# One inference step of a streaming encoder layer on one Trainium2 core: running sums two steps behind their loads, decay factors three steps later in the first group, the second norm's rows stored by ScalarE, and another input for an early Silu

## The chip, the core and the metric

The kernel runs on one core of one Trainium2 chip. The metric is the time of one execution on the device, in microseconds (us). A profile of one execution shows, for each engine, when it worked and what ended each of its waits: TensorE (PE, matmuls; PEld, its weight loads), VectorE (DVE), ScalarE (ACT), GpSimd (POOL) and SyncE (SP), whose queue issues most of the transfers.

## What is computed

One layer for 2048 prompt tokens and 64 sample tokens, 1024 features, everything in float32. `layer` of the reference, cut to its course:

```python
mod = (c_act @ w_ada + b_ada)[:, None, :]
sh1, sc1, gt1, sh2, sc2, gt2 = jnp.split(mod, 6, -1)
h = rmsnorm(x, g1) * (1 + sc1) + sh1
u, q, k, v, o, gates = jnp.split(h @ w_in, cuts, -1)
pool_out, pool_buf_new = pool_mixer(u, pool_buf, start, w_pool, s_pool)
hs, C, n, m = mlstm_seq(q, k * HEAD_DIM ** -0.5, v, ig, lf, C, n, m)   # 4 heads, chunks of tokens
hs = hs * lax.rsqrt(jnp.mean(hs * hs, -1, keepdims=True) + EPS) * g_head * jax.nn.sigmoid(o)
x = x + gt1 * (jnp.concatenate([pool_out, hs], -1) @ w_out)
h2 = rmsnorm(x, g2) * (1 + sc2) + sh2
up = h2 @ w_up                      # then a causal conv of width 3, halves a and g
x = x + gt2 * ((jax.nn.silu(g) * a) @ w_down)
y = rmsnorm(x, g_final)
```

## The kernel before

Tokens run along the free dimension. The first part (the attention half) takes four groups of tokens, 512 each, the last with the 64 sample tokens as well. Every matrix product is made of three passes over operands that are split in a high and a low part, so TensorE has most of the work.

A group goes through the projection of v and the gates (`proj_v`), four heads of q, k and o (`proj_qko`), four pooling projections and the output projection (`outproj`). Beside these matmuls run smaller pieces of work, each written as a generator. They stand in lists `bg[0]` to `bg[5]`, and `gemm` takes the next step of one of them (`tick(i)`) at fixed places among its matmuls. A `yield` in a generator is the end of such a step, so one more `yield` puts what follows one step later. A list is a queue: what is behind a generator in its list waits until it is done. `drain(i)` takes all that is left of a list at once. In the attention half, behind group 0's first projections, a scheduler of the framework then orders each engine's instructions by when it thinks that they can start, so the program's order is not quite the engines'. In the second half (FFN) the written order of the compute engines stands.

The pieces that matter here:

- `ada` (lines 175 to 230) makes one of the modulation vectors per group (the sample's and the prompt's) as running sums on VectorE: 16 blocks of `w_ada` (128x512) are loaded into tiles `raw` by SP (line 192), and each is multiplied into two accumulators (line 205 for a new pair, line 207 else), 32 instructions. Later groups (`first=False`) load three blocks ahead, and the block three further behind each step. There are four tiles `raw`, so a fifth load waits until the sums of the first block are done. It stands in `bg[3]`, three ticks to a projection.
- `up_sums` (lines 866 to 902, `bg[4]`) adds and subtracts blocks of `w_up` (lines 892 to 896) and stores them (`wsum`, line 881, SP) for the FFN.
- `gate_rows` (lines 1167 to 1244, `bg[0]`) turns the gates into decay factors: `CL` by a transpose (line 1229), a copy (line 1233) and three exponentials (line 1235), and four yields later `GL` by a matmul (line 1241) and a copy (line 1242). Right after the first head's three projections stands `drain(0)` (line 1455).
- `lstm` (lines 1265 to 1356) is one head's memory: `at` (lines 1278, 1281, 1300), `kw` (line 1289), the states `st` (line 1314) and the output `nd` (lines 1320 to 1323).
- `norm_h` (lines 730 to 749, `bg[1]` of the last group) normalizes the first FFN group's rows: it loads sixteen half rows of `x2d` into ten tiles (line 738), scales and shifts each (line 726 on VectorE, line 728 on ScalarE) and stores it to `h2d` (line 746, SP). Half rows 10 to 15 go into tiles whose first content must have been stored.

SP's queue is in order: a transfer that waits (for a tile to come free, or for the result that it stores) holds back all behind it. Besides the named ones it carries the weights that TensorE takes, `hl_kept` to `wt` (line 374), 512 KB each.

Between the halves, line 1970 runs a Silu on one column of `V`, into a column of `RF` that later work overwrites; its result is not used. The first Silu whose result is used is that of line 1665. ScalarE must have the table of a function loaded before it runs (ACT_TABLE_LOAD). `V` holds the small vectors and is loaded at the kernel's start; `UC` (line 1495) is a tile of the FFN that GpSimd sets to zero (line 1496).

Of the kernel before, what the change touches and what calls it, by code (L numbers as in the profile page):

```python
# [11 lines left out]
AF = mybir.ActivationFunctionType  # L12
# [14 lines left out]
FH = FT // 2  # L27
# [36 lines left out]
def tile_layer(ctx: ExitStack, tc: tile.TileContext, xT, vecs, cst, rst, rowv, w_mod, w_ada, w_qkou, w_v, w_pool,  # L64
               w_out, w_up, w_down, w_quad, st_C, st_pool, yT, o_pool, o_C, o_m, o_conv):
    nc = tc.nc
    act, dve, pool, pe = nc.scalar, nc.vector, nc.gpsimd, nc.tensor
# [19 lines left out]
    def m2_ps():  # L87
        return bank("m2")
# [9 lines left out]
    def scr():  # L98
        return sp.tile([P, TMAX], F32, tag="scr", name="scr")
# [22 lines left out]
    def big(tile):  # L122
        return tile.bitcast(F32).rearrange("p a t -> p (a t)")
# [11 lines left out]
    V = cp.tile([P, NV], F32, tag="V", name="V")  # L135
# [27 lines left out]
    def raw_tile():  # L163
        return wp.tile([P, WN], F32, tag="raw", name="raw", bufs=RB)
# [10 lines left out]
    def ada(m, first):  # L175


        todo = [(j, k) for j in range(2) for k in range(KD)]
        src = [w_ada[m - 2, k, :, j * 512:(j + 1) * 512] for j, k in todo]
        got = {}  # L180

        def load(i):
            if first:

                if i % 2 == 0 and i < len(todo):
                    w = a1.tile([P, 4, 256], F32, tag="w4", name="w4", bufs=5).rearrange("p (a b) c -> p a (b c)", a=2)
                    for d in range(2):
                        got[i + d] = w[:, d]
                        tc.keep_in_program_order(nc.sync.dma_start(out=w[:, d], in_=src[i + d]))
            elif i < len(todo):  # L190
                got[i] = raw_tile()[:, :512]
                nc.sync.dma_start(out=got[i], in_=src[i])
        lead = 4 if first else 3
        for i in range(lead):
            load(i)
        yield
        accs = []
        for i, (j, k) in enumerate(todo):
            if k == 0:
                acc = [a1.tile([P, 512], F32, tag="acc", name="acc", bufs=4) for _ in range(2)]  # L200
                accs += acc
            w = got.pop(i)
            for s in range(2):
                if k == 0:
                    dve.tensor_scalar(out=acc[s], in0=w, scalar1=CA[:, k, s:s + 1], scalar2=None, op0=ALU.mult)
                else:
                    dve.scalar_tensor_tensor(out=acc[s], in0=w, scalar=CA[:, k, s:s + 1], in1=acc[s],  # L207
                                             op0=ALU.mult, op1=ALU.add)
            load(i + lead)
            yield  # L210
        yield

        pt = m2_ps()
        for c, acc in enumerate(accs):
            pe.matmul(pt[32 * c:32 * c + 32, :], ones[:, 0:32], acc, start=True, stop=True)
        MR = scr()
        dve.tensor_copy(MR[:, :512], pt)
        yield
        yield
        pt = m2_ps()  # L220
        for n in range(4):
            pe.transpose(pt[:, n * P:(n + 1) * P], MR[:, n * P:(n + 1) * P], ident)
        for j in range(2):
            bia = V[:, V_BA + m * 8 + 4 * j:V_BA + m * 8 + 4 * j + 4]
            dve.tensor_tensor(out=MOD[:, m, 4 * j:4 * j + 4],
                              in0=pt.rearrange("p (n c t) -> p n c t", n=4, c=4)[:, :, 2 * j:2 * j + 2, 0],
                              in1=bia.unsqueeze(2).broadcast_to([P, 4, 2]), op=ALU.add)
        if m == 4:
            scale_cols(G2, V_G2, 4, 0, KD)
        yield  # L230

    def scale_cols(G, v0, m, k0, n):
        dve.scalar_tensor_tensor(out=G[:, k0:k0 + n], in0=MOD[:, m, k0:k0 + n], scalar=1.0,
                                 in1=V[:, v0 + k0:v0 + k0 + n].unsqueeze(2).broadcast_to([P, n, 2]),
                                 op0=ALU.add, op1=ALU.mult)
# [6 lines left out]
    for g in range(NG):  # L242
        o = Grp()
# [219 lines left out]
    def mx_tile(k):  # L463
        return beside(mx, "mx", k)
# [91 lines left out]
    h2d = dr.tile([KD, P, FT], F32, tag="h2d", name="h2d")  # L556
# [3 lines left out]
    RF = cp.tile([P, 16], F32, tag="RF", name="RF")  # L560
# [71 lines left out]
    for g in range(NFG):  # L632
        o = Grp()
# [87 lines left out]
    def normed(x, k, t0, w, rb):  # L721

        for (a, b, s) in ((t0, min(t0 + w, TP), 0), (max(t0, TP), t0 + w, 1)):
            if a < b:
                a, b = a - t0, b - t0
                dve.scalar_tensor_tensor(out=x[:, a:b], in0=x[:, a:b], scalar=G2[:, k, s:s + 1], in1=rb[:, a:b],  # L726
                                         op0=ALU.mult, op1=ALU.mult)
                act.activation(x[:, a:b], x[:, a:b], AF.Identity, bias=sh2(k, s))

    def norm_h(o, rows, scr):  # L730

        todo = [(t0, k) for t0 in (o.t0, o.t0 + FH) for k in range(KD)]
        xs = []

        def load(i):
            t0, k = todo[i]
            xs.append(rows[i % 10])
            nc.sync.dma_start(out=xs[i], in_=x2d[k, :, t0:t0 + FH])
        for i in range(8):
            load(i)  # L740
        box = []
        for h in range(2):
            yield from bcast_cols(RS2, o.t0 + h * FH, FH, box, lambda dt=F32: rows[10 + h] if dt == "rb" else scr(dt))
        for i, (t0, k) in enumerate(todo):
            normed(xs[i], k, t0, FH, box[i // KD])
            nc.sync.dma_start(out=h2d[k, :, t0:t0 + FH], in_=xs[i])
            yield
            if i > 1 and i + 6 < len(todo):
                load(i + 6)
# [109 lines left out]
    if True:  # L859
# [44 lines left out]
        def rows_of(o):  # L904

            xs = []
            for k in range(0, KD, 2):
                t = big(mx_tile(k))
                for i in (0, 1):
                    xs.append(t[:, i * TMAX:i * TMAX + o.T])  # L910
                    if o.g > 1:
                        nc.sync.dma_start(out=xs[-1], in_=xT[k + i, :, o.t0:o.t0 + o.T])
            return xs
# [253 lines left out]
        def gate_rows(o, gt, cols):  # L1167
# [58 lines left out]
            for (a, b, n, s) in o.tsegs:  # L1226
# [3 lines left out]
                for qn in range(4):  # L1230
# [2 lines left out]
                        dve.tensor_copy(CL[:n, a:b, qn, :], src)  # L1233
                    else:
                        act.activation(CL[:n, a:b, qn, :], src, AF.Exp)
            for _ in range(4):
                yield
            pb = m2_ps()
            for (a, b, n, s) in o.tsegs:
# [184 lines left out]
        for o in groups:  # L1424
# [3 lines left out]
            if o.g > 0:  # L1428
                bg[3].append(ada(2 + o.g, False))
                tick(3)  # L1430
# [15 lines left out]
            if o.last:  # L1446
                xs = [t[:, j * FH:(j + 1) * FH] for t in [big(mx_tile(k)) for k in range(4)] for j in range(3)]
            else:
                xs = rows_of(groups[o.g + 1])
# [45 lines left out]
    UC = f1.tile([P, 2 * NF, 2], F32, tag="UC", name="UC")  # L1495
# [471 lines left out]
    ET = mybir.EngineType  # L1967
    fctx.enter_context(tc.manual_schedule(engines={ET.PE, ET.Activation, ET.DVE, ET.Pool}))
    x3, ssum = [], None
    act.activation(RF[:, 0:1], V[:, 0:1], AF.Silu)  # L1970
    bg[5].append(down_sums())
    for o in fgroups:
        Bo = B[o.g]
# [244 lines left out]
```

## Time and profile before

| What | Value |
|---|---|
| time, median of 3 (lowest to highest) | 2201.76 us (2200.48 to 2202.48) |
| the profiled execution: its time, its span | 2205.02 us, 2203.2 us |
| granted clock of TensorE, mean over the span | 0.996 |
| PEld busy | 2067.4 us |
| DMA engines, moved bytes and mean rate | 521.67 MB, 237 GB/s |
| L442, matmuls of the attention half (out of `hl`) | 397.5 us busy, 1920 instructions |
| L207, running sums on VectorE, `raw` tiles | 60.5 us busy, 84 instructions, 29.2 us idle before them |
| L1547, matmuls of the FFN's first products | 889.7 us busy, 5544 instructions |

The profile covers one execution. Its span runs from the first instruction to the last, and the 1.8 us around it (2205.02 - 2203.2) belong to no instruction. A row of the groups names the line, the engine, the operation, `out<-in` and the shapes, then how often, the busy time, the mean duration in ns, and the idle time of the engine just before these instructions with what ended it. Durations of matmuls overlap, so the distance between two starts says more than the sum of durations.

The groups of tokens start (first matmul of `proj_v`) at about 222 us (group 1), 404 us (group 2) and 590 us (group 3); the FFN's first product of its first pair ends at about 809 us.

### The profile page before, as it was taken

The page shows a single profiled execution, that of the slowest core. Times are in us where ns is not written, and L with a number is a line of the kernel's source. Part 1 is how long each engine was busy: PE and PEld are TensorE (multiplying, and loading weights), DVE is VectorE, ACT ScalarE, POOL GpSimd, SP SyncE. Part 2 cuts the span into 40 slices and gives each one's busy share as a digit, 9 for nine tenths or more (in the row PEclk, how much of TensorE's full clock was granted, in tenths as well). Part 3 has the DMA queues.
Part 4 walks back from the last instruction along what each step waited for, and adds up shares of the span by engine and source line. Part 5 has one row for each costly group of instructions (what it writes and reads, how often), then busy time and mean ns, then how long its engine had stood idle before and what let it go on. Part 6 is the DMA issues. An engine that isn't in the chain of part 4 may idle for free. (4 is left out here: it accounts for less than half of the span.)

```text
span 2203.2 us, 38338 instructions
## 1 busy us (share of the span) xinstructions
PE 2178.9 (99%) x13708; PEld 2067.4 (94%) x13708; DVE 1630.4 (74%) x2996; ACT 1038.8 (47%) x2024; POOL 262.1 (12%) x546
## 2 busy tenths in 40 slices
PE   8999999999999999999999999999999999999998
PEld 7888888888899999999999999999999999999998
DVE  4887659577765768787958677676757597888885
ACT  3553335244343446464636444545435356554454
POOL 0010001001000100000101220101111331121112
PEclk9999999999999999999999999999999999999999
DMA  9977986997898686667646877777569786665562
GB/s 336 357 251 257 340 287 230 321 325 244 287 327 271 208 298 221 207 199 243 208 157 215 294 230 235 232 208 220 180 185 277 219 247 179 182 175 181 157 200 79
DMA packets 304191, 521.67 MB, mean 237 GB/s; under 512 B 27480, under 2 KB 131288, under 8 KB 304000
## 3 DMA queue, kind: packets, MB, share of 16 engines
q1 hardware_dynamic: 283008, 482.74, 67.0%
q10 hardware_dynamic: 11776, 28.09, 3.4%
q0 software_dynamic: 9216, 8.39, 3.0%
q8 instruction: 108, 1.77, 0.3%
q14 instruction: 83, 0.68, 0.1%
HBM read 408.36 MB, written 127.52 MB: 243 GB/s over the span
## 5 line engine op out<-in xcount | busy, mean ns | idle before, releaser
L1547 PE MATMUL mm<-hx,wt 128*128 128x352 f32 x5544 | 889.7, 321 | 3.0 <-DVE wt L388 1.5
L1547 PEld LDWEIGHTS mm<-hx,wt 128*128 128x128 f32 x5544 | 880.3, 188 | 7.5 <-DVE wt L388 4.3
L442 PE MATMUL mm<-hl,wt 128*128 128x512 f32 (+2 forms) x1920 | 397.5, 359 | 2.0 <-DMA wt<-hl_kept 2.0
L2061 PE MATMUL mm<-av,wt 128*128 128x352 f32 (+2 forms) x2400 | 385.2, 321 | 0.4 <-DVE av L1701 0.3
L385 ACT ACTIVATE wt<-raw 128x512 fp32r<-128x512 f32 (+3 forms) x510 | 288.8, 579 | 202.2 <-PE mm L2061 59.6
L2061 PEld LDWEIGHTS mm<-av,wt 128*128 128x128 f32 x2400 | 380.6, 188 | 2.5 <-DVE av L1701 0.6
L388 DVE TENSOR_TENSOR wt<-raw,wt 128x512 fp32r<-128x512 f32 (+3 forms) x510 | 323.6, 649 | 69.7 <-ACT wt L385 69.0
L442 PEld LDWEIGHTS mm<-hl,wt 128*128 128x128 f32 x1920 | 314.2, 189 | 49.7 <-issue 4.4
L442 PE MATMUL mm<-mx,wt 128*128 128x512 f32 (+1 forms) x960 | 186.6, 353 | 0.0
L442 PEld LDWEIGHTS mm<-mx,wt 128*128 128x128 f32 x960 | 158.7, 188 | 25.1 <-ACT mx L1403 1.1
L385 ACT ACTIVATE wt<-wt 128x512 fp32r<-128x512 f32 x176 | 110.6, 628 | 120.4 <-DMA wt<-wsum 109.1
L1535 DVE SCALAR_TENSOR_TENSOR tg<-eg,V,tg 128x704 f32<-128x704 f32 (+1 forms) x132 | 125.7, 952 | 35.3 <-ACT tg L1530 32.8
L388 DVE TENSOR_TENSOR wt<-wt 128x512 fp32r<-128x512 f32 x176 | 119.3, 686 | 30.3 <-ACT wt L385 30.0
L2078 DVE SCALAR_TENSOR_TENSOR x<-mm,MOD,x 128x352 f32<-128x352 f32 (+4 forms) x152 | 77.9, 559 | 79.2 <-PE mm L2061 79.2
L1535 DVE SCALAR_TENSOR_TENSOR ta<-ea,V,ta 128x704 f32<-128x704 f32 (+1 forms) x132 | 125.6, 951 | 7.5 <-ACT ta L1530 5.0
L1808 PE MATMUL mm<-av,wt 128*128 128x352 f32 x576 | 94.4, 321 | 0.0
L1808 PEld LDWEIGHTS mm<-av,wt 128*128 128x128 f32 x576 | 91.8, 188 | 0.0
L207 DVE SCALAR_TENSOR_TENSOR acc<-raw,CA,acc 128x512 f32<-128x512 f32 x84 | 60.5, 746 | 29.2 <-DMA raw<-w_ada 29.1
L1555 DVE TENSOR_TENSOR eg<-mm,u 128x352 f32<-128x352 f32 x154 | 69.9, 466 | 15.2 <-ACT u L1634 9.3
L1665 ACT ACTIVATE tg<-tg 128x704 f32<-128x704 f32 (+1 forms) x66 | 52.3, 793 | 60.9 <-DVE tg L1535 60.7
L1613 ACT ACTIVATE u<-mm 128x352 f32<-128x352 f32 x66 | 30.4, 461 | 91.9 <-PE mm L1547 59.3
L1139 PE MATMUL mm<-wt,hl 128*128 128x256 f32 (+1 forms) x576 | 70.9, 282 | 0.0
(328 smaller groups left out, 2287.7 us busy)
## 6 DMA issues: line engine op xcount, KB each, us to landing
wt<-hl_kept SPq DMA_DIRECT2D x108, 512.0 KB, 5.9
raw<-w_up SPq DMA_DIRECT2D x198, 256.0 KB, 3.8
wt<-wsum SPq DMA_DIRECT2D x176, 256.0 KB, 4.6
wt<-wsplit SPq DMA_DIRECT2D x88, 512.0 KB, 4.8
w<-w_up SPq DMA_DIRECT2D x88, 256.0 KB, 5.6
wsum<-w SPq DMA_DIRECT2D x44, 512.0 KB, 6.5
wsplit<-wt SPq DMA_DIRECT2D x44, 512.0 KB, 4.6
raw<-w_down SPq DMA_DIRECT2D x88, 256.0 KB, 3.6
```

What stands on the lines that cost most here:

```text
L207: dve.scalar_tensor_tensor(out=acc[s], in0=w, scalar=CA[:, k, s:s + 1], in1=acc[s], op0=ALU.mult, op1=ALU.add)
L385: act.activation(u.w[:, 0, :u.n], u.raw[:, :u.n], AF.Copy)
L388: dve.tensor_tensor(out=u.w[:, 1, :u.n], in0=u.raw[:, :u.n], in1=u.w[:, 0, :u.n].bitcast(F32), op=ALU.subtract)
L442: pe.matmul(ps[bi][:, :hi - lo], U[:, a, k % 4 * P:(k % 4 + 1) * P], mv[k][:, b, lo:hi], start=(at == 0 and pi == 0), stop=(k == order[-1] ...
L1139: pe.matmul(ps[ti][:n, :cols], h[4 * kh + k4][:, b, lo:lo + n], U[:, a, k4 % 2 * cols:(k4 % 2 + 1) * cols], start=(kh == 0 and k4 == 0 and ...
L1535: dve.scalar_tensor_tensor(out=t[:, :E], in0=ext[:, j:j + E], scalar=wc(j, f), in1=t[:, :E], op0=ALU.mult, op1=ALU.add)
L1547: pe.matmul(ps[:, :FH], U[:, a, kc * P:(kc + 1) * P], Bo.at(nm, kc, b), start=(first and kc == 0 and pi == 0), stop=(kc == 3 and pi == 2), ...
L1555: dve.tensor_tensor(out=ext[:, d:d + b - a], in0=ps[:, a:b], in1=u[:, a:b], op=ALU.add)
L1665: act.activation(self.tg[:, :E], self.tg[:, :E], AF.Silu)
L1808: pe.matmul(ps, U[:, x, w:w + P], quad.d[nm][z], start=(start and k == 0 and pi == 0), stop=(k == 1 and pi == 2), skip_group_check=not start)
L2061: pe.matmul(ps[i][:, :hi - lo], U[:, a, k % 4 * P:(k % 4 + 1) * P], av[k](b, lo, hi), start=(k == 0 and (a, b) == PASSES[0]), stop=(k == n ...
L2078: dve.scalar_tensor_tensor(out=x3[n][:, a:b], in0=ps[i][:, a - lo:b - lo], scalar=gt2(n, s), in1=x3[n][:, a:b], op0=ALU.mult, op1=ALU.add)
```

## The change

```diff
@@ ada
         for i in range(lead):
             load(i)
-        yield
+        for _ in range(1 if first else 3):
+            yield
         accs = []
@@ norm_h
             normed(xs[i], k, t0, FH, box[i // KD])
-            nc.sync.dma_start(out=h2d[k, :, t0:t0 + FH], in_=xs[i])
+            act.dma_start(out=h2d[k, :, t0:t0 + FH], in_=xs[i])
             yield
@@ gate_rows
-            for _ in range(4):
+            for _ in range(4 if o.g else 7):
                 yield
             pb = m2_ps()
@@ ahead of the FFN
-    act.activation(RF[:, 0:1], V[:, 0:1], AF.Silu)
+    act.activation(RF[:, 0:1], UC[:, 0, 0:1], AF.Silu)
```

The sums of groups 1 to 3 begin two steps later behind their first three loads; every further load and sum keeps its distance to the others. The sixteen stores to `h2d` go from SP's queue to ScalarE's. In group 0 three more yields stand ahead of the matmul of line 1241. The Silu between the halves reads `UC`, which exists only there, and no longer `V`. The first part adds a line, so from line 198 on the changed kernel's line numbers are higher by one.

What stands on the engines now, at three places. First, VectorE at the start of group 2, where the gates' rows (L1182 to L1217 before, L1183 to L1218 now) are worked out; `w4` are the blocks of `up_sums`, `acc` and `raw` those of `ada`. Before:

```order
L1182 SCALAR_TENSOR_TENSOR scr_4340<-scr_4303 4x512
L207 SCALAR_TENSOR_TENSOR acc_4445<-raw_4469,CA_127,acc_4445 128x512
L207 SCALAR_TENSOR_TENSOR acc_4446<-raw_4469,CA_127,acc_4446 128x512
L1189 SCALAR_TENSOR_TENSOR scr_4303<-scr_4303,scr_4340 4x512
L207 SCALAR_TENSOR_TENSOR acc_4445<-raw_4479,CA_127,acc_4445 128x512
L1192 SCALAR_TENSOR_TENSOR scr_4397<-RST_146,scr_4303 4x512
L1200 SCALAR_TENSOR_TENSOR M_208<-scr_4303,M_208,scr_4302 4x512
L1204 TENSOR_TENSOR scr_4340<-scr_4302,scr_4397 4x512
L207 SCALAR_TENSOR_TENSOR acc_4446<-raw_4479,CA_127,acc_4446 128x512
L1209 TENSOR_TENSOR scr_4302<-scr_4397,M_208 4x512
L892 TENSOR_TENSOR w4_4456<-w4_4456 128x256
```

Now:

```order
L1183 SCALAR_TENSOR_TENSOR scr_4340<-scr_4303 4x512
L893 TENSOR_TENSOR w4_4450<-w4_4450 128x256
L894 TENSOR_TENSOR w4_4450<-w4_4450 128x256
L896 TENSOR_TENSOR w4_4450<-w4_4450 128x256
L897 TENSOR_TENSOR w4_4450<-w4_4450 128x256
L1190 SCALAR_TENSOR_TENSOR scr_4303<-scr_4303,scr_4340 4x512
L1193 SCALAR_TENSOR_TENSOR scr_4397<-RST_146,scr_4303 4x512
L1201 SCALAR_TENSOR_TENSOR M_208<-scr_4303,M_208,scr_4302 4x512
L1205 TENSOR_TENSOR scr_4340<-scr_4302,scr_4397 4x512
L1210 TENSOR_TENSOR scr_4302<-scr_4397,M_208 4x512
```

The running sums are gone from among the gates' rows, and a whole block of `up_sums` (first named `w4_4456`, now `w4_4450`) stands ahead of them. Four more sums than before now stand at the end of group 1. SP's queue moved with it: behind the store of `w4_3374` the two loads of `w4_4450` are issued, where it was three loads of `raw`.

Second, VectorE some 15 rows further, around the copy to `CL` (L1233, now L1234) and that to `GL` (L1242, now L1243). Before:

```order
L205 TENSOR_SCALAR acc_4596<-raw_4541,CA_127 128x512
L205 TENSOR_SCALAR acc_4597<-raw_4541,CA_127 128x512
L207 SCALAR_TENSOR_TENSOR acc_4596<-raw_4562,CA_127,acc_4596 128x512
L207 SCALAR_TENSOR_TENSOR acc_4597<-raw_4562,CA_127,acc_4597 128x512
L1199 COPY M_208<-M_208 4x1
L1233 COPY CL_4528<-m2_4530 128x4x4
```

Now:

```order
L206 TENSOR_SCALAR acc_4676<-raw_4574,CA_127 128x512
L206 TENSOR_SCALAR acc_4677<-raw_4574,CA_127 128x512
L1234 COPY CL_4520<-m2_4522 128x4x4
L208 SCALAR_TENSOR_TENSOR acc_4676<-raw_4590,CA_127,acc_4676 128x512
L208 SCALAR_TENSOR_TENSOR acc_4677<-raw_4590,CA_127,acc_4677 128x512
L1243 COPY GL_4521<-m2_4579 128x16
```

The pair that opens the second pair of accumulators still stands ahead of the copy to `CL`, and its load (`raw_4574`) is now issued behind the store of `w4_3832` on SP, where `raw_4541` and `raw_4562` were issued ahead of it.

Third, SP's queue in group 3, at `norm_h`: `mx` tiles are loaded from `x2d` and stored to `h2d`. Before:

```order
L746 DMA h2d_133<-mx2_6325 128x352
L881 DMA wsum_129<-w4_6635 512x1x256
L738 DMA mx1_6324<-x2d_132 128x352
L746 DMA h2d_133<-mx2_6325 128x352
L738 DMA mx1_6324<-x2d_132 128x352
L746 DMA h2d_133<-mx3_6326 128x352
L374 DMA wt_7190<-hl_kept_128 128x2x512
L881 DMA wsum_129<-w4_6793 512x1x256
L738 DMA mx1_6324<-x2d_132 128x352
```

Now:

```order
L739 DMA mx0_6323<-x2d_132 128x352
L739 DMA mx1_6324<-x2d_132 128x352 x2
L375 DMA wt_7190<-hl_kept_128 128x2x512
L882 DMA wsum_129<-w4_6625 512x1x256
L882 DMA wsum_129<-w4_6785 512x1x256
L739 DMA mx1_6324<-x2d_132 128x352
```

No store to `h2d` stands between the loads any more; of the last three half rows two are issued ahead of the two stores of `wsum`, and the last one behind them. On ScalarE the sixteen stores stand one or two instructions behind the L729 whose result they store.

On no engine does a row of group 0 move, but for the Silu of line 1970: it stood on ScalarE among the squares of the kernel's first rows, and stands now near the end of the attention half, between a square of the output projection's rows (L626) and a split of weights (L386), with the ACT_TABLE_LOAD ahead of it that stood at L1665. Nothing is computed otherwise than before.

## The prediction

> **What bounds the kernel now.** I read the page's busy times first, then TensorE's waits, then for each wait the timelines of the engine named and of the queue behind it.
>
> ```profile
> PE 2178.9 (99%) x13708; PEld 2067.4 (94%) x13708; DVE 1630.4 (74%) x2996; ACT 1038.8 (47%) x2024; POOL 262.1 (12%) x546
> ```
>
> TensorE is busy for 99% of the span, and the change takes no matmul away. So only its waits can be gained, and every microsecond that another engine saves counts for nothing unless one of these waits ends on it. The waits that an edit can reach (seconds after the colon: sum, count, longest, us):
>
> ```profile
> PE mm L442 <- DMA wt<-hl_kept: 2.0, 3, 1.2
> PE m L1320 <- DVE st L1314: 1.9, 1, 1.9
> PE m L1241 <- ACT CL L1235: 1.3, 1, 1.3
> ```
>
> That is 5.2 us in all. In group 2, TensorE waits three times within 9 us (start, duration, instruction, the wait in brackets):
>
> ```profile
> 434.36 2.35 PE L442 MATMUL mm<-hl,wt 128*128 128x512 f32 x9 [0.54 <-DMA wt<-hl_kept]
> 436.55 0.29 PE L1241 MATMUL m<-CL,C 128*128 128x16 f32 x2
> ...
> 438.88 1.63 PE L442 MATMUL mm<-hl,wt 128*128 128x512 f32 x6 [1.23 <-DMA wt<-hl_kept]
> ...
> 443.09 1.13 PE L1309 MATMUL m<-va,kw 128*128 128x129 f32 x8 [0.33 <-DVE kw L1289]
> ...
> 445.89 0.28 PE L1320 MATMUL m<-st,q 128*128 128x129 f32 x1
> ```
>
> In group 3 it waits once, for the state of the last `lstm`, and its clock falls behind that wait:
>
> ```profile
> 670.38 0.39 PE L1321 MATMUL m<-va,at 128*128 128x129 f32 x2
> ...
> 672.69 0.49 PE L1320 MATMUL m<-st,q 128*128 128x129 f32 x2 [1.92 <-DVE st L1314]
> 673.26 3.23 PE L442 MATMUL mm<-hl,wt 128*128 128x256 f32 x12
> ```
>
> ```profile
> 642.84 1.74 PE L442 MATMUL mm<-hl,wt 128*128 128x256 f32 x12
> ```
>
> ```profile
> 673.00:676.50 3.50, 3.50 (x18) 0.51 0.84 317
> ```
>
> The last row is TensorE by windows: length, busy time, instructions, granted clock, DMA share, GB/s. At a clock of 0.51 the twelve matmuls take 3.23 us where the same twelve take 1.74 at 642.84: the wait costs 1.92 and 1.49 more behind it.
>
> **Part 1, sums two steps later (groups 1 to 3).** What held the two weights of group 2 stands on VectorE and on SP's queue:
>
> ```profile
> 416.29 1.41 DVE L207 SCALAR_TENSOR_TENSOR acc<-raw,CA,acc 128x512 f32<-128x512 f32 x2 [3.36 <-DMA raw<-w_ada]
> ...
> 432.90 0.15 DVE L1233 COPY CL<-m 128x16 f32<-128x16 f32 x1
> ...
> 442.26 0.68 DVE L1289 TENSOR_TENSOR kw<-m,CL 128x512 f32<-128x512 f32 x1
> ...
> 444.72 0.42 DVE L895 TENSOR_TENSOR w<-w 128x256 f32<-128x256 f32 x1
> 445.06 0.35 DVE L1314 SCALAR_TENSOR_TENSOR st<-SP,GL,m 128x129 f32<-128x129 f32 x1
> ```
>
> ```profile
> 428.16 0.56 SPq L881 DMA_DIRECT2D wsum<-w  x1
> ...
> 429.50 0.93 SPq L374 DMA_DIRECT2D wt<-hl_kept  x1
> 430.52 0.60 SPq L192 DMA_DIRECT2D raw<-w_ada  x1
> ...
> 432.49 0.83 SPq L374 DMA_DIRECT2D wt<-hl_kept  x1
> ```
>
> ```profile
> SPq L881 <- DVE w L896: 4.6, 1, 4.6
> ```
>
> SP's queue stands for 4.6 us on one store of `up_sums`, until VectorE's L896 is done and the store goes out at 428.16; the weights for 434.36 and 438.88 are issued behind it. VectorE came to that block late because of sums of `ada` among the gates' rows, at the wait of 3.36 above all. In the changed order five of those sums leave the stretch between L1182 and that L896, and two rows of another block come in. A pair of sums takes 1.41 us, so five make 3.5; a row of a block moves the next start by 445.06 - 444.72 = 0.34, so two make 0.7. The store moves 2.8 us earlier, to about 425.4. The wait of 3.36 itself I leave where it is: the block of `up_sums` that now stands ahead of the gates' rows waits for its own load, issued at the place in SP's queue where a `raw` load stood, and these two land alike:
>
> ```profile
> wt<-hl_kept SPq DMA_DIRECT2D x12, 512.0 KB, 6.4
> raw<-w_ada SPq DMA_DIRECT2D x12, 256.0 KB, 6.7
> w<-w_up SPq DMA_DIRECT2D x8, 256.0 KB, 6.4
> ```
>
> Behind the store stands one load more than before, 0.6 to issue, so the weights move 2.2 earlier; the first needs 0.54 and the second 1.23 plus the 0.54 no longer lost ahead of it, 1.77: both waits close. What they are worth is a little more than their idle time. From 670.38 to 672.69 are 2.31 us, of which the pair of L1321 fills some 0.22, which leaves 2.09 against 1.92: 0.17 for each restart. So the three waits are 0.54 + 1.23 + 0.33 + 3 x 0.17 = 2.6 us.
>
> What is late next: the `raw` load that opens the second pair of accumulators now stands behind the store instead of ahead of it. It goes out at about 428.3 (430.52 less 2.2), lands 6.7 later at 435.0, its pair of sums (L206) takes at most 0.9, and only then, in the same queue, comes the copy to `CL`, at 435.9, 3.0 later than the 432.90 of before. TensorE will want L1241 at 436.55 - 0.7 = 435.85; with some 0.5 for the copy and its exponentials they end at 436.4, so 0.5 may be lost there. The sums that follow stand ahead of `kw`: the last load that it needs has five issues between it and the first, at 0.6 to 0.9 each, so it goes out at about 432.4 and lands 6.7 later at 439.1; two sums and a row of `up_sums` take 1.41 + 0.34, and `kw` starts at 440.9. From `kw` to the state were 445.06 - 442.26 = 2.80, with one sum more now 3.47: the state starts at 444.37, ends at 444.7, and TensorE, which without waits would want it at 445.89 - 2.6 = 443.3, gets it at 444.8. The gain is 445.89 - 444.8 = **1.1 us**, with bounds of 0 (CL later by another us takes it all) and 2.6 (those loads land faster than the median). I take 1.1 because it uses medians of this very stretch. Groups 1 and 3 have no wait of TensorE at their sums; I give them 0.
>
> **Part 2, stores of `norm_h` on ScalarE.**
>
> ```profile
> 671.78 0.59 DVE L726 SCALAR_TENSOR_TENSOR mx<-mx,G,mx 128x352 f32<-128x352 f32 x1 [2.22 <-DMA mx<-x2d]
> 672.29 0.35 DVE L1314 SCALAR_TENSOR_TENSOR st<-SP,GL,m 128x129 f32<-128x129 f32 x1
> ```
>
> ```profile
> 659.98 0.57 SPq L881 DMA_DIRECT2D wsum<-w  x1
> ...
> 664.39 0.64 SPq L881 DMA_DIRECT2D wsum<-w  x1
> 665.08 0.62 SPq L738 DMA_DIRECT2D mx<-x2d  x1
> ```
>
> ```profile
> mx<-x2d SPq DMA_DIRECT2D x6, 176.0 KB, 4.1
> ```
>
> The state that TensorE waits for stands on VectorE behind the last L726, and this behind the last load of `x2d`, issued at 665.08 after stores to `h2d` that wait for ScalarE, a weight and a store of `wsum`. Now no such store is ahead of it, only the two stores of `wsum`, of which the first went out at 659.98; with the transfers that stood between them and the load gone, I put the load near 660. It lands after the median 4.1 to the 6.7 that the last one took (671.78 - 665.08): 664 to 667. VectorE then has no wait of 2.22, and the state is ready about 2.1 earlier than 672.29 + 0.35 = 672.64, that is 670.5, when TensorE comes to it (670.38 + 0.22 = 670.6). Gain: 1.92 + 0.17 = **2.1 us**, and **1.5** for the clock, together 3.6. If the load moves by less than 2 us, the gain falls in proportion; at 0 it is rival E.
>
> The clock's 1.5 hang on this wait: it fell right behind 1.92 us of idling, while 1.3 at L1241 and 1.23 at 438.88 left it up. [...]
>
> The price of the stores is on ScalarE:
>
> ```profile
> L728 ACT ACTIVATE mx<-mx,MOD 128x352 f32<-128x352 f32 x16 | 9.0, 590 | 13.6 <-DVE mx L726 13.6
> L854 ACTq DMA_DIRECT2D Bd<-fscr x56: 326/326/444, 894.9 to 1591.5; - x56
> ```
>
> ```profile
> 641.68 0.71 ACT L1248 ACTIVATE q<-mm 128x256 f32<-128x256 f32 x2 [6.79 <-PE mm L442]
> ```
>
> A store that ScalarE issues takes it 0.33 to 0.44 us (second row: least, median, most in ns), so sixteen are 5.3 to 7.0. It idles 13.6 us ahead of these L728, so I cost them 0; uncovered they cost up to 7.0.
>
> **Parts 3 and 4.** The yields in group 0 move no row on any engine: TensorE's wait of 1.3 at L1241 stays, since what is left of that generator at `drain(0)` is issued there either way. Cost 0; were it to do what the numbers say, at most 1.3 + 0.17 = 1.5 would go. The Silu:
>
> ```profile
> 830.62 1.28 ACT L1665 ACT_TABLE_LOAD   x1
> 831.91 0.80 ACT L1665 ACTIVATE tg<-tg 128x704 f32<-128x704 f32 x1
> ```
>
> ```profile
> 772.26 0.69 ACT L625 ACTIVATE scr<-scr 128x576 f32<-128x576 f32 x1 [0.37 <-DVE scr L615]
> 775.06 0.63 ACT L385 ACTIVATE wt<-raw 128x512 fp32r<-128x512 f32 x1 [2.11 <-PE mm L442]
> ```
>
> The table's load of 1.28 leaves 830.62, where no wait of TensorE stands, and goes with the Silu of one column to 772.95 (772.26 + 0.69), into an idle time of 2.11, which leaves 0.8 for that Silu. Cost 0 both ways; uncovered, 1.3. [...]
>
> **The sum**: 1.1 + 2.1 + 1.5 = 4.7 us. Against the profiled execution, 2205.02 (a span of 2203.2 and 1.8 around it), that is 2200.3. That execution is 3.3 above the median of 2201.76; I carry the difference over: 2201.76 - 4.7 = **2197.1 us**. If the 3.3 are themselves such waits, the median has less to gain, which is one reason for the range's upper end.
>
> **The rivals.**
> - *B, group 2 gives all*: the loads of `raw` land within 5 us, `kw` is in time, 2.6 + 3.6 = 6.2, 2195.6. For it: the queue gets room where 3.36 of waiting was. Against: the load really stands behind the store now.
> - *C, group 2 gives nothing*: the wait on `raw` only moves ahead of `CL`, and the decay factors end on TensorE's path. 3.6 gained: 2198.2. For it: the order shows that pair ahead of the copy. Against: the median landing just fits.
> - *D, the clock falls anyway*: 4.7 - 1.5 = 3.2 gained, 2198.6. Against: 3.23 against 1.74 right behind the wait.
> - *E, group 3's wait comes back*, from another load or from ScalarE's L728 late: only 1.1 gained, 2200.7. For it: ten tiles for sixteen half rows.
> - *F, slower*: the stores stand in ScalarE's queue ahead of the evacuations of TensorE's banks. The evacuation at 641.68 had waited 6.79 for TensorE, and that slack must be eaten by the stores, each waiting for its L728; if ScalarE falls behind by those 6.8, TensorE stops for the issues, 16 x 0.39 (between 0.33 and 0.44) = 6.2, and group 3 gains nothing: 2201.76 + 6.2 - 1.1 = 2206.9.
> - *The yields work after all*: 1.5 more. The order excludes it, so it gets no chance of its own.
>
> **How the numbers follow.** Forecast A 0.46, B 0.18, C 0.14, D 0.05, E 0.10, F 0.07. A measurement of this kernel tells about 0.2%, 4.4 us, from no change: 2197.4 and 2206.2 are the bounds. A lies at the first of them, with a spread of some 1.3 either way for its two estimates: 0.29 of it below, 0.17 above. Faster: 0.29 + 0.18 = 0.47. Within: 0.17 + 0.14 + 0.05 + 0.10 = 0.46. Slower: F, 0.07. The range runs from B with its spread, 2194.6, to E with some, 2201.6; it leaves out F and the ends of B and E.
>
> **What would show it.** Right: no wait for `hl_kept` between 430 and 440, a wait (or none) of TensorE for `st` or `CL` near 436 to 445 instead; no wait at L1320 near 670 and a clock of 1.00 there; the wait at L1241 of group 0 still 1.3; an ACT_TABLE_LOAD near 773 with L386 on time behind it. Wrong: a fall of the clock without a long wait (D), a second wait of VectorE for `x2d` (E), or waits of TensorE for a bank near 640 to 665 (F).

## The result: slower by 0.2%, and the profile after

| | before | changed |
|---|---|---|
| median of 12 runs (lowest to highest) | 2200.49 us (2197.29 to 2205.87) | 2204.20 us (2202.07 to 2208.22) |
| ratio, 95% interval | | 1.0020 (1.0012 to 1.0028) |
| the profiled execution: its time, its span | 2205.02, 2203.2 us | 2206.83, 2205.1 us |

The forecast was 2197.1, in a range to 2201.6. The changed kernel takes 3.7 us more than the one before. Note the profiled execution of before: it is 4.5 above the median, and two of the twelve runs took longer.

TensorE's waits in the profile of the changed kernel, between 100 and 810 us (after the colon: sum, count, longest in us; lines from 198 on are one higher than before):

```profile
PE m L1310 <- DVE at L1301: 2.7, 1, 2.7
PE m L1310 <- DVE kw L1290: 1.7, 3, 0.7
PE mm L443 <- DMA wt<-hl_kept: 1.4, 2, 0.9
PE m L1299 <- ACT at L1279: 1.1, 1, 1.1
PE m L216 <- DVE kw L1290: 0.8, 1, 0.8
PE m L1352 <- DVE nd L1341: 0.7, 1, 0.7
```

The wait for `st` at L1320 (now L1321) is gone, as forecast, and three others stand at its place in group 3. On TensorE's timeline:

```profile
664.41 1.42 PE L1299 MATMUL m<-q,k 128*128 128x128 f32 x10 [1.06 <-ACT at L1279]
...
667.58 1.06 PE L216 MATMUL m<-acc,ones_r 128*32 128x512 f32 x8 [0.76 <-DVE kw L1290]
...
673.05 0.91 PE L1310 MATMUL m<-va,kw 128*128 128x129 f32 x4 [2.74 <-DVE at L1301]
```

That is 4.56 us where before had 1.92 and the slow clock behind it. The clock stayed up this time, by TensorE's windows (length, busy time, granted clock, DMA share, GB/s):

```profile
669.00:673.00 4.00, 1.31 (x11) 1.00 0.82 241
673.00:676.50 3.50, 3.45 (x25) 1.00 1.00 320
```

What VectorE, SP and ScalarE did then, each from its own timeline:

```profile
666.85 0.88 DVE L1290 TENSOR_TENSOR kw<-m,CL 128x512 f32<-128x512 f32 x2
671.81 0.58 DVE L727 SCALAR_TENSOR_TENSOR mx<-mx,G,mx 128x352 f32<-128x352 f32 x1 [4.08 <-DMA mx<-x2d]
672.31 0.80 DVE L1301 TENSOR_TENSOR at<-at,m 128x512 f32<-128x512 f32 x2
```

```profile
659.63 2.03 SPq L375 DMA_DIRECT2D wt<-hl_kept  x1
661.75 1.82 SPq L882 DMA_DIRECT2D wsum<-w  x2
663.67 1.41 SPq L739 DMA_DIRECT2D mx<-x2d  x1
```

```profile
666.49 5.05 ACTq L747 DMA_DIRECT2D h2d<-mx  x2
671.59 0.59 ACT L729 ACTIVATE mx<-mx,MOD 128x352 f32<-128x352 f32 x1 [5.16 <-DMA h2d<-mx]
```

VectorE stands for 4.08 us at the last row of `norm_h`, whose half row of `x2d` was issued at 663.67 and landed some 8.1 later, at the same 671.8 as before. And this row now stands ahead of `at` (L1301); before, `at` (L1300) was done ahead of it and only the state stood behind it:

```profile
667.56 0.81 DVE L1300 TENSOR_TENSOR at<-at,m 128x512 f32<-128x512 f32 x2
...
671.78 0.59 DVE L726 SCALAR_TENSOR_TENSOR mx<-mx,G,mx 128x352 f32<-128x352 f32 x1 [2.22 <-DMA mx<-x2d]
```

So a load that is no earlier holds back more. ScalarE stands too: its second store of the pair at 666.49 goes out at 671.21.

Group 2 has the same waits as before in other places:

```profile
432.74 2.34 PE L443 MATMUL mm<-hl,wt 128*128 128x512 f32 x9 [0.59 <-DMA wt<-hl_kept]
...
436.88 1.63 PE L443 MATMUL mm<-hl,wt 128*128 128x512 f32 x6 [0.86 <-DMA wt<-hl_kept]
...
441.50 0.68 PE L1310 MATMUL m<-va,kw 128*128 128x129 f32 x4 [0.73 <-DVE kw L1290]
```

```profile
433.38 0.89 DVE L206 TENSOR_SCALAR acc<-raw,CA 128x512 f32<-128x512 f32 x2 [6.83 <-DMA raw<-w_ada]
434.18 0.17 DVE L1234 COPY CL<-m 128x16 f32<-128x16 f32 x1
```

The two waits for `hl_kept` shrank from 1.77 to 1.45. VectorE's wait for `raw` now stands right ahead of the copy to `CL`, as rival C had it, and takes 6.83; among the gates' rows, where it was 3.36 before, VectorE waits 2.56 for `w_up`.

### The profile page after: what moved, and what is told of

It is laid out like the page before. It is cut to its first block, busy times and chain, and to the rows that moved or that the text cites. A ratio compares the mean times of both kernels' runs of the same rounds, so it can differ in the third digit from the quotient of the medians.

```text
span 2205.1 us, 38344 instructions
## 1 busy us (share of the span) xinstructions
PE 2178.3 (99%) x13708; PEld 2067.3 (94%) x13708; DVE 1630.2 (74%) x2996; ACT 1038.4 (47%) x2024; POOL 261.5 (12%) x546
## 3 DMA queue, kind: packets, MB, share of 16 engines
q8 instruction: 108, 1.77, 0.3%
## 5 line engine op out<-in xcount | busy, mean ns | idle before, releaser
L386 ACT ACTIVATE wt<-raw 128x512 fp32r<-128x512 f32 (+3 forms) x510 | 289.0, 579 | 210.2 <-PE mm L2062 56.2
L386 ACT ACTIVATE wt<-wt 128x512 fp32r<-128x512 f32 x176 | 110.5, 628 | 139.0 <-DMA wt<-wsum 119.2
L1140 PEld LDWEIGHTS mm<-wt,hl 128*128 128x128 f32 x576 | 69.3, 188 | 1.0 <-issue 0.6
```

The source lines that it names most:

```text
L386: act.activation(u.w[:, 0, :u.n], u.raw[:, :u.n], AF.Copy)
L1140: pe.matmul(ps[ti][:n, :cols], h[4 * kh + k4][:, b, lo:lo + n], U[:, a, k4 % 2 * cols:(k4 % 2 + 1) * cols], start=(kh == 0 and k4 == 0 and ...
```

## The experiments

All times are medians, each against runs of the kernel before on the same chip. The last three columns are TensorE's waits in the one profile of each run, added up from its timeline: group 2 (430 to 465), group 3 (655 to 675), output projection (750 to 790). "c" marks waits at which the granted clock fell to half, for 3.4 us each time and for 6.8 in stores_pool.

| run | this / before, us | ratio (95%) | group 2 | group 3 | outproj |
|---|---|---|---|---|---|
| before, first profile | | | 2.3 | 1.92 c | 0 |
| before_again | 2205.09, one run | | 3.6 | 1.66 c | 0 |
| the change | 2204.20 / 2200.49 | 1.0012 to 1.0028 | 2.9 | 4.56 | 0 |
| sums_only | 2201.60 / 2200.31 | 0.9998 to 1.0015 | 2.7 | 0.13 | 0 |
| stores_only | 2202.33 / 2200.31 | 0.9999 to 1.0017 | 2.9 c | 2.21 c | 0 |
| yields_silu | 2199.84 / 2200.31 | 0.9991 to 1.0009 | 2.8 | 1.08 | 0 |
| no_stores | 2199.97 / 2200.15 | 0.9992 to 1.0010 | 2.7 | 0 | 0 |
| stores_pool | 2205.45 / 2198.80 | 1.0017 to 1.0035 | 2.6 | 5.39 c | 0 |
| last8_stores | 2200.79 / 2199.46 | 0.9998 to 1.0016 | 2.9 | 1.33 | 0 |
| first8_stores | 2201.27 / 2199.67 | 0.9996 to 1.0014 | 2.6 | 0.71 | 0 |
| late_rows | 2200.05 / 2200.07 | 0.9996 to 1.0013 | 1.9 | 1.61 | 0 |
| stores_late_rows | 2202.19 / 2200.07 | 0.9998 to 1.0018 | 2.9 c | 2.61 | 0 |
| all_late_rows | 2204.40 / 2200.07 | 1.0015 to 1.0033 | 3.8 | 2.71 c | 0 |
| fewer_updates | 2205.33 / 2199.46 | 1.0018 to 1.0042 | 3.0 | 0 | 3.6 |
| fewer_updates_stores | 2203.45 / 2199.46 | 1.0011 to 1.0031 | 2.8 | 0.75 | 3.4 |
| paced_updates | 2204.56 / 2200.15 | 1.0008 to 1.0025 | 3.0 | 0 | 3.5 c |
| paced_updates_all | 2207.17 / 2200.15 | 1.0018 to 1.0040 | 2.9 | 2.97 | 3.4 c |
| sums_half_blocks | 2199.13, one run | | 2.9 | 0.10 | 0 |
| paced_group2 | 2202.43, one run | | 1.5 | 0.90 | 3.9 c |
| paced_2_and_3 | 2199.47 / 2199.67 | 0.9992 to 1.0010 | 2.5 c | 0 | 0 |

### The parts by themselves

```diff
 sums_only: only the first hunk of the change
 stores_only: only the second
 yields_silu: only the third and fourth
 no_stores: the first, third and fourth
```

> Part 1 alone (the sums of groups 1 to 3 two steps later). The changed kernel took 3.7 us longer than the one before (2204.2 against 2200.5). Theory S, the stores: the loss comes from ScalarE's queue in group 3, so this kernel is at the time of before or up to 1.1 us faster (ratio 0.9995 to 1.000), and TensorE shows no wait over 0.5 us between 655 and 675. Theory A, the sums: of the 3.7 at least 1.8 are here (ratio 1.0008 to 1.0017), with waits of TensorE at L1310 in group 2 (near 440 and 461) and the lost 0.9 us between 265 and 290.

> Part 2 alone (the stores to h2d on ScalarE). Theory S: 2 to 4 us slower than before (ratio 1.0009 to 1.0018), with TensorE's waits near 661 to 673 for ScalarE (L1279 or L1278) and for the last load of x2d. Theory A: not slower, down to the 3.6 us that the prediction gave this part (ratio 0.9984 to 1.000); what group 3 lost in the changed kernel came from the sums' later place there.

> Parts 3 and 4 alone (three more yields in group 0, the Silu on UC). Theories S and A: within 0.5 us of before (ratio 0.9998 to 1.0002); the wait at L1241 of group 0 is still there. A third theory, U: what the profile of the changed kernel shows as 0.5 us of L1665's place (near 830) and the shorter start are real, which gives -2.6 to +0.5 us.

> Parts 1, 3 and 4 without part 2: a second measurement of the sums. If the sums cost 1 to 1.5 us, as part 1 alone gave (1.3, with 0 in its interval), the ratio is 1.0004 to 1.0008; if that was scatter, 0.9997 to 1.0003. Its wait at L1320 near 670 is under 0.3 us as in part 1 alone, and group 2 has the waits of 0.7 at L1310 near 440 and 461.

Parts 3 and 4 show no cost, as S and A had it; the interval reaches 2 us either way, so a small gain (U) is not excluded. Part 1 alone took 1.3 us longer with 0 in its interval, and in the second measurement, with parts 3 and 4, it took nothing: that it costs time is not shown. Part 2 alone took 2.0 longer, with 0 just inside. The clearest comparison is the change against no_stores: 3.7 us of loss with part 2, none (1.0001) without, and in group 3 4.56 us of waits with it, none without. So the loss is part 2's. The place fits: between the same two matmuls of L442, those that start at 650 and 685 in the profile of before, pass 31.4 us in no_stores and 36.6 in the changed kernel (32.8 in yields_silu, 35.2 in before), while the other stretches up to the FFN differ by under half a microsecond between these two. The FFN itself scatters, 1394 to 1398 us over the profiles.

In no_stores the last row of `norm_h` stands behind `at`, and nothing waits, though its load went out at 664.70, later than the 663.67 of the changed kernel:

```profile
666.34 0.80 DVE L1301 TENSOR_TENSOR at<-at,m 128x512 f32<-128x512 f32 x2
...
669.72 0.57 DVE L727 SCALAR_TENSOR_TENSOR mx<-mx,G,mx 128x352 f32<-128x352 f32 x1
```

By the medians part 2 costs more on top of part 1 (3.7) than alone (2.0), but the intervals overlap. A reason would be that part 1 had by itself taken away the wait at L1320: in sums_only it is 0.13 us, in no_stores 0. No step of the prediction had that. The times did not fall with it, and where it was paid for is not shown; no_stores has 0.97 us at L1352 in group 1, which before doesn't have.

For part 1 in group 2, SP's and TensorE's timelines of sums_only:

```profile
426.12 0.62 SPq L375 DMA_DIRECT2D wt<-hl_kept  x1
```

```profile
432.33 2.34 PE L443 MATMUL mm<-hl,wt 128*128 128x512 f32 x9 [0.41 <-DMA wt<-hl_kept]
```

and of before_again:

```profile
427.46 0.95 SPq L374 DMA_DIRECT2D wt<-hl_kept  x1
```

```profile
432.64 2.34 PE L442 MATMUL mm<-hl,wt 128*128 128x512 f32 x9 [1.40 <-DMA wt<-hl_kept]
```

The weight is taken 6.2 us after its issue (432.33 - 426.12) in the one, 5.2 in the other: issued earlier, it was underway longer, behind one load of `w_up` more.

### Which queue takes the stores

```diff
 stores_pool
-            nc.sync.dma_start(out=h2d[k, :, t0:t0 + FH], in_=xs[i])
+            pool.dma_start(out=h2d[k, :, t0:t0 + FH], in_=xs[i])
 last8_stores (first8_stores with i < 8)
+            (act if i > 7 else nc.sync).dma_start(out=h2d[k, :, t0:t0 + FH], in_=xs[i])
```

> The stores to h2d on GpSimd's queue, all else as before. In the run with part 2 alone ScalarE stood at stores (up to 3.95 us) whose completion semaphore was still held by an older transfer of SP, and the part cost 2.0 us (2202.33 against 2200.31), though within its interval of 0. Theory Q, ScalarE's queue: the cost is what stands behind such a store on ScalarE; GpSimd has nothing behind it, so this kernel is not slower than before (ratio 0.9990 to 1.0000) and ScalarE has no wait for h2d or w_up at L728 between 650 and 672. Theory L, the loads: VectorE's rows L726 are placed earlier, ahead of L217 and L1300, and their loads land no earlier; then VectorE still stands 2 us or more for mx<-x2d near 661 to 670, TensorE waits behind it, and 1 to 3 us are lost (ratio 1.0005 to 1.0014).

> The kernel before once more, for a second profile. The first one's execution took 2205.02 us, 4.7 above the median of 27 (2200.31). If that execution was an unlucky one in group 3, TensorE's wait at L1320 near 670 is 1.1 us here as in the run with parts 3 and 4, or less, and its clock stays at 1.00 there; if it was a usual one, the wait is 1.9 and the clock falls to about 0.5 behind it.

> Only the last eight of the sixteen stores to h2d on ScalarE; no load of x2d waits for these, and VectorE's order stays exactly that of before. Theory Q (a store that ScalarE cannot issue yet, since its completion semaphore is held by an older transfer, holds the exponentials and evacuations behind it): most of part 2's 2.0 us are here, 1 to 2 us slower (ratio 1.0004 to 1.0010), with TensorE waiting for ScalarE near 660 to 670. Theory L (VectorE's order and its loads): as before, ratio 0.9997 to 1.0003, and the only wait of TensorE between 650 and 675 is the 1.1 to 1.9 us at L1320.

> Only the first eight of the sixteen stores on ScalarE, the complement of the last eight (which cost 1.3 us by the clock, 0 in its interval, and no wait of TensorE beyond that of before). The last six loads of x2d wait for stores 0 to 5, and VectorE's order is nearly that of part 2 alone. Theory L (order of VectorE's rows, with loads that come no earlier): the cost of part 2 is here: TensorE waits 1.5 us or more between 655 and 675 behind a row L726 or a block of up_sums that waits for its load, ratio 1.0004 to 1.0014. Theory Q (ScalarE standing at stores): the stores in the dense part, from 655 on, are SP's again, so the time is that of before, ratio 0.9996 to 1.0003.

On GpSimd, which has no other work between 651 and 675, the stores cost 6.7 us by the medians, the most of the three queues. So ScalarE's standing is not needed for a loss, and Q as the only cause falls. That the stores on ScalarE lose time in the same way is a likeness of the waits, not shown by this run. VectorE's timeline there shows what TensorE's wait of 5.39 (L1288, behind L217) came from:

```profile
656.98 0.58 DVE L726 SCALAR_TENSOR_TENSOR mx<-mx,G,mx 128x352 f32<-128x352 f32 x1 [4.06 <-DMA mx<-x2d]
...
662.60 0.58 DVE L726 SCALAR_TENSOR_TENSOR mx<-mx,G,mx 128x352 f32<-128x352 f32 x1 [4.37 <-DMA mx<-x2d]
```

Two rows of `norm_h`, each ahead of the attention's rows, stand 4 us each for a load of `x2d`. ScalarE does stand at stores as well; in stores_only its timeline has

```profile
668.05 1.65 ACTq L746 DMA_DIRECT2D h2d<-mx  x2
669.74 1.24 ACT L728 ACTIVATE mx<-mx,MOD 128x352 f32<-128x352 f32 x2 [3.95 <-DMA h2d<-mx]
```

The first of these stores went out at 668.05, and SP's next load at 667.99. What such a store waits for shows in the trace of the changed kernel: of the pair at 666.49 the second went out at 671.21, and its record has it wait for a store of `wsum` that SP had issued at 663.02 and that landed at 671.14. In stores_only an L728 behind another of these stores, at 656.78, had its wait of 2.45 us ended by a load of `w_up`. So in these two profiles ScalarE stood at its stores for transfers of SP that they have nothing to do with.

With half of the stores moved, neither half shows a cost that the time can tell from 0 (1.3 and 1.6 us by the medians), and TensorE's wait in group 3, 1.33 and 0.71, is not above that of before in either. By the waits, neither L, which wanted the cost in the first eight, nor Q, which wanted it in the last eight, is borne out. The times decide nothing: their intervals hold 0 and the cost that was expected.

The profile of before_again is once more one of an unusually long time (2205.09 against 2198.80), with 1.66 us and the fall of the clock. Of all 150 timed runs of before, 8 are above 2204. yields_silu, with the same rows in group 3 and a usual time, has 1.08 and no fall.

### Later rows for the norm

```diff
 late_rows, behind load(i + 6); stores_late_rows with part 2, all_late_rows with the whole change
+            for _ in range(0 if i < 4 else 3): yield
```

> The kernel before with three more yields behind each half row from the fifth on in norm_h, so that the last rows L726 stand later on VectorE: one ahead of the last lstm's first state instead of two, and four behind its states instead of none. Stores stay on SP. Theory L (what TensorE waits for in group 3 is VectorE's queue, standing at a row L726 whose load of x2d waits for a tile, and so for a store): the wait at L1320 near 670 (1.1 to 1.9 us in three profiles) goes; 1 us faster than before, up to 3.5 where the clock no longer falls (ratio 0.9984 to 0.9996). If something else holds the state, the wait stays and the ratio is 0.9998 to 1.0005.

> Part 2 with the same late rows. Theory L: the 2.0 us of part 2 alone go with them, since ScalarE's standing at stores costs nothing by itself; ratio 0.9984 to 1.0002, no wait of TensorE over 0.5 us between 655 and 675. Theory Q (ScalarE's queue): 1 to 2 us slower than before stay (ratio 1.0004 to 1.0010), with TensorE waiting behind L1248 or L1278 of ScalarE.

> The whole change with the same late rows. Theory L: of the change's 3.7 us the 2 to 3 that arise in group 3 go, and what the sums cost in groups 1 and 2 stays, 0 to 1.3 (ratio 0.9994 to 1.0006); the wait of 2.74 at L1310 near 670 is gone. Theory Q: the waits behind ScalarE near 663 and 667 stay (1.06 and 0.76 in the changed kernel), ratio 1.0008 to 1.0015.

Theory L, as it stood here, fell: the times stayed where they were. In late_rows one row L726 still stood ahead of the state and waited 2.75 us. In the two others blocks of `up_sums` stood in its place, ahead of `at`, and waited for their own loads. VectorE in all_late_rows:

```profile
668.36 0.42 DVE L893 TENSOR_TENSOR w<-w 128x256 f32<-128x256 f32 x1 [4.66 <-DMA w<-w_up]
...
669.16 0.80 DVE L1301 TENSOR_TENSOR at<-at,m 128x512 f32<-128x512 f32 x2
```

It is the same wait with another load's name. That led to the next theory, B: the stretch has more to load than the DMA engines move in it.

### Fewer bytes in the full stretches

```diff
 fewer_updates (fewer_updates_stores with part 2): up_sums slower in heads 0 and 1 of the last group
-            if at in ups and not quiet:
+            if at in ((1, 4) if ease else ups) and (not quiet or o.last):
...
+                ease[:] = [1] if o.last and hd < 2 else []
 paced_updates (paced_updates_all with the whole change; paced_group2 and paced_2_and_3 alike)
+            if at in (pace[0] if pace else ups) and not quiet:
...
+                pace[:] = [(1, 4) if hd < 2 else (1, 2, 3, 4, 6, 7)] if o.last else []
 sums_half_blocks, with part 1
+                nc.sync.dma_start(out=got[i][:, :256], in_=src[i][:, :256])
+            w = got.pop(i)[:, :256].unsqueeze(1).broadcast_to([P, 2, 256])
```

> The kernel before with up_sums slowed in the last group's first two heads (two steps per projection instead of four) and made up for in that group's pooling, where the DMA engines are half idle; stores on SP. Theory B (between 630 and 680 the DMA engines are full, so whichever row stands at the head of VectorE's queue waits for a load, and with it the state): with about half of the 768 KB per block gone from this stretch the waits of VectorE for x2d fall under 1 us each, TensorE's wait at L1320 goes, and 1 to 2 us are gained (ratio 0.9990 to 0.9996), unless the pooling, where VectorE is busy for nine tenths, loses some of it. If the wait is one of order alone, it stays at 1.1 us or more and the ratio is 0.9998 to 1.0005.

> Part 2 on top of the slowed up_sums. Theory B: the 2.0 us of part 2 alone go too; no wait of TensorE over 0.5 us between 650 and 680, ratio 0.9990 to 0.9998. Theory Q: ScalarE still stands at stores, 1 to 2 us above the run with slowed up_sums and stores on SP.

> The kernel before, up_sums slowed in the last group's first two heads as in the run with fewer updates, but made up for in its last two heads (six steps per projection instead of four) and not in the pooling. Theory B: TensorE's wait in group 3 goes (or falls under 0.5 us) as it did there, and the 3.6 us that VectorE and ScalarE lost at 753 to 782 don't come; 1 to 2 us faster than before (ratio 0.9990 to 0.9997). If it is VectorE's load and not the DMA engines that decides, waits come up near 690 to 720 and the ratio is 0.9998 to 1.0010.

> The whole change with the same pace of up_sums. Theory B: of the changed kernel's 4.6 us of waits between 663 and 673 less than 1 is left, and of its loss (ratio 1.0020) what the sums cost in groups 1 and 2 stays: 0.9996 to 1.0010. Theory Q (ScalarE's queue): waits behind ScalarE (L1278, L1248 by the lines of before) of 1 us or more are still there, ratio 1.0008 to 1.0015.

> Part 1 alone, but each later group's block of w_ada is loaded only in its first half (128 KB instead of 256), and the sums use that half twice; the other half of those vectors is left out. In group 2 the engines' order stays but for the place of one or two sums. Theory B, bandwidth: the weights behind the late store went out 1.3 us earlier in the run with part 1 alone and still landed at the same time, because more bytes stand ahead of them; with 256 KB less ahead of the second weight it lands 0.7 us earlier, and TensorE's two waits for hl_kept near 432 and 436 fall from 0.41 and 0.88 us to under 0.3 and 0.3. Theory O, order: what counts is only when SP issues them; both waits stay as they were, within 0.2 us.

> The kernel before, up_sums slowed in group 2's first head (two steps per projection instead of four) and made up for in its third. Theory B for group 2: with one block (768 KB) less between 410 and 440 the two waits for hl_kept (1.0 to 1.4 us each) fall under 0.5 us each; something else may then be late, L1309 at most. If only the order of issue counts, they stay within 0.3 us of that.

> The kernel before with up_sums slowed in group 2's first head and in the last group's first two heads, and made up for in the later heads with enough steps that nothing of it is left for the output projection (in the paced run before, a block was left over and cost 4.9 us near 785). Theory B: the waits for hl_kept near 432 and 437 go (as they did with group 2 paced), that at L1320 near 670 falls under 0.5 us, and nothing is lost near 785: 1 to 2.5 us faster than before, ratio 0.9988 to 0.9996. If every load taken from one stretch is missed in the next, 0.9998 to 1.0005.

In group 3 theory B holds with the stores on SP: in fewer_updates, paced_updates and paced_2_and_3 TensorE has no wait there at all. The windows of fewer_updates and no_stores (length; busy time of PE, PEld, DVE, ACT, POOL; clock, DMA share, GB/s) show where the bytes went, and a limit of the theory:

```profile
630.00:655.00 25.00, 25.00 (x188) 23.74 (x187) 16.45 (x43) 14.22 (x42) 1.87 (x2) 1.00 0.74 233
655.00:675.00 20.00, 20.00 (x151) 17.97 (x151) 12.24 (x36) 7.67 (x27) 1.49 (x1) 1.00 0.95 316
```

```profile
630.00:655.00 25.00, 24.94 (x182) 23.33 (x182) 20.28 (x54) 13.06 (x40) 1.87 (x2) 1.00 0.95 321
655.00:675.00 20.00, 20.00 (x152) 17.96 (x151) 13.89 (x37) 9.17 (x29) 0.00 (x0) 1.00 0.93 306
```

fewer_updates loads at 0.74 ahead of the place and so has its rows ready. But no_stores has 0.95 there and no wait either. So a full stretch does not make the wait by itself. What fits both is that it makes loads late, and that the order of VectorE's rows decides whether one of them stands ahead of what TensorE needs; no run changed only one of the two.

With the stores on ScalarE the cure works less: 0.75 us are left in fewer_updates_stores (against 2.21), but 2.97 in paced_updates_all, where VectorE stood 3.14 for `x2d` and 2.18 for `w_up`. There B's forecast of less than 1 was missed.

And no version gained time. What `up_sums` did not do in the heads it did later: in the output projection waits of 3.4 to 3.9 us came up (fewer_updates: 1.3, 0.9 and 1.5 behind L388, L1403 and L385). In paced_updates a block was left over for that place; with more steps in paced_2_and_3 no load of it is left for there and nothing is lost, but group 2 still waits, and the time is that of before.

In group 2 the two waits for `hl_kept` went in paced_group2, paced_2_and_3 and sums_half_blocks (which leaves out half of each later block of `w_ada`), as B expected. `kw` took their place, 1.50, 2.53 and 2.87 us, behind sums that wait for `raw`:

```profile
PE m L1309 <- DVE kw L1289: 2.5, 1, 2.5
```

That is the only wait listed for paced_2_and_3 between 400 and 810. Over all runs group 2 loses 1.5 to 3.8 us in whatever order its rows and transfers stand.

## Why the prediction was wrong

- **Part 2, group 3: the step that failed.** It put the last load of `x2d` "near 660", landing after 4.1 to 6.7 us. It went out at 663.67, behind a weight whose issue took 2.03 and two stores of `wsum`; that is 1.4 earlier than the 665.08 of before, not 5, and it took 8.1, so it landed no earlier at all. One of the two stores stood until 663.02, the last 0.7 us by SP's waits, for the landing of a load of `x2d` issued at 658.24. The transfers that are gone from SP's queue were not gone from the DMA engines: the sixteen stores still move their 176 KB each, and the engines' share is 0.91 before and 0.98 now from 655 to 675. (From 630 to 655 it is 1.03 before and 0.91 now, so that fuller engines made the landing late is not shown.) Rival E, with 0.10, had the wait come back, but at the size of before; TensorE's waits there are 4.56 now against 1.92. For that the prediction would have needed VectorE's new order. It kept the order of before: that the last row of `norm_h` now stands ahead of `at` is not in it.
- **The baseline.** Of the 3.6 us to be gained in group 3, the lower clock's 1.5 and part of the 1.92 are probably not in the median: yields_silu shows 1.08 and a full clock at a usual time, while both profiles of before are of long executions. The length of a wait alone does not decide whether the clock falls, as the last section shows. The prediction carried the sum over to the median and named this risk, but only for the range's upper end.
- **Part 1, group 2.** The store of `wsum` did move as worked out (issued at 428.16 before and 423.93 now; of these 4.23 us 1.67 are this execution's lead, as VectorE's first gates' row shows, 411.48 and 409.81; that leaves 2.6 against 2.8 forecast). The copy to `CL` came as forecast too: 434.18 + 1.67 = 435.85, against 435.9. What failed is "both waits close": the load more behind the store took 1.0 to issue instead of 0.6, so the first weight went out 1.5 earlier (426.29 + 1.67 = 427.96, against 429.50) instead of 2.2, and TensorE took it 6.45 us after its issue, where it was 4.86 (432.74 - 426.29 and 434.36 - 429.50). The prediction moved the issue and kept the time from there to the landing. Rival C's gain of nothing held for this group, but TensorE did not wait for the decay factors as in C: it waited for the weights and for `kw`.
- **Part 1, group 3**: a term put at 0 that took the 1.1 to 1.9 at L1320 away, by a changed order of rows. It does not show in the time.
- **Parts 3 and 4** came as forecast. The wait at L1242 of group 0 is there in every run (0.33 to 1.31 us). The table is loaded at 774.30, for 1.28, and the split behind it starts as soon as TensorE lets it:

```profile
774.30 1.28 ACT L1971 ACT_TABLE_LOAD   x1
775.59 0.20 ACT L1971 ACTIVATE RF<-UC 128x1 f32<-128x1 f32 x1
776.34 0.63 ACT L386 ACTIVATE wt<-raw 128x512 fp32r<-128x512 f32 x1 [0.54 <-PE mm L443]
```

- **Rival F**, slower by the stores on ScalarE, had the sign, with 0.07, and 2206.9 where 2204.20 was measured; that is luck. Its mechanism was a queue of issues ahead of evacuations at 16 x 0.39. What the profiles show is different: ScalarE standing at its stores (5.16 us at the longest in the changed kernel), and above all VectorE standing for loads (4.08 at the last row of `norm_h`).

Settled by the runs: the loss is part 2's, and stores on a queue other than ScalarE's lose time as well. By one profile of each run: it arises between 655 and 675. Argued, not shown: that it comes from the stores no longer pacing SP's queue, so that the loads pile up. Open: how much of the 4.56 us is ScalarE's own standing. The 1.06 at L1299 is behind its exponentials (L1279), and so are 0.89 in stores_late_rows; no run took that standing away by itself.

## What to carry to other kernels

A transfer that went to another queue left the first queue's order here, not the DMA engines: with these at a share of 0.98 from 655 to 675, a load issued 1.4 us earlier landed at the same time. Where VectorE feeds TensorE and also does background work on loads, look up which background row stands ahead of the needed one in the changed order; one late load there cost 4.08 us here, where the issue of a store on ScalarE took 0.33 (median of the sixteen). And check whether the profiled execution is a usual one before a wait in it is booked as a gain.

## What was not expected of the hardware

The clock. Behind waits of 1.66 (before_again), 1.92 (before) and 2.21 us (stores_only) it fell to about half for 3.4 us, and so it did behind 2.71 (all_late_rows), while it stayed at 1.00 behind 2.74 (the changed kernel) and 2.97 us (paced_updates_all). In stores_only, with a wait from 662.29 to 664.50:

```profile
664.50:668.00 3.50, 3.50 (x15) 0.51 1.07 383
```

and in paced_updates_all, from 663.41 to 666.38:

```profile
666.50:670.00 3.50, 3.50 (x26) 1.00 1.01 377
```

So here the length of a wait alone doesn't decide it, and what else does is not shown by these runs. In the clock record of before the slow stretch starts at 673.05, 0.36 us behind the end of the wait of 1.92, and lasts 3.41 us.
